# Attention weights built with keys on the partitions from a second set of scores, in a two-layer hybrid trunk

## The chip, the cores and the metric

The kernel runs on one core of a Trainium2 chip. The metric is the device time of one execution in microseconds (us). The engines are named as in the profile: PE (matrix products; PEld is its loading of the stationary operand), DVE (vector), ACT (activation), POOL and SP. The last two, in this kernel, mostly issue DMAs.

## The reference

Two layers on 512 tokens of 1024 features, all float32. Each layer is half a SwiGLU, a mixer and half a SwiGLU, every one on a normalised input and added to the stream. The mixer makes one projection of the normalised input, splits its columns over three groups (a short convolution, a gated recurrence, and attention) and projects the joined results back. The change is in the attention, which is this, for 8 heads of 64 features:

```python
qh = rms_norm(heads(q), q_gain) * (HEAD_DIM ** -0.5)
kh = rms_norm(heads(k), k_gain)
vh = heads(v)
log_f = jax.nn.log_sigmoid((f_logit + f_bias).astype(f32))
cum = jnp.cumsum(log_f, axis=1).transpose(0, 2, 1)
# for each block of 128 queries:
s = einsum('bhqd,bhkd->bhqk', qb, kh) + (cb[..., :, None] - cum[..., None, :])
s = jnp.where(qpos[:, None] >= kpos[None, :], s, MASK_VALUE)
p = jax.nn.softmax(s, axis=-1)
o = einsum('bhqk,bhkd->bhqd', p, vh)
```

The term `cb` is the same for all keys of a query, so it does not change the softmax; only minus `cum` of the key is needed.

## The kernel before, in words

Products are made at float32 accuracy out of float32r ones: every operand is split into a rounded part and a remainder (`hi` and `lo`, `PH` and `PL`, `yh` and `yl`), and the product is the sum of high by high, high by low and low by high. The dense products (`mm3`, lines 376, 382 and 383) do this with three matmuls each. Weight rows come by DMA into `st` (2 buffers), ACT writes the high part and DVE the remainder into `hl` (3 buffers, lines 362 and 363), and PE multiplies.

A layer's mixer begins with the recurrence (`hgrn`), beside which the columns q, k of the attention are projected (`fox_qkv`). Then comes the stretch that the change touches, in which two generators are interleaved by hand. One is `rest()`: what is left of the projection of v, the convolution (`conv`), and most of the output projection (`most`). The other is `attend`, made by `fox_attend`. The tuple `BESIDE` says how many steps of `rest()` stand before each step of `attend`; a step of `rest()` is 12 matmuls of 512 columns in the convolution and 9 in the output projection. `follow("p", ...)` fixes the order of most of these matmuls on PE. The tile scheduler orders the other engines.

`attend` takes the 8 heads in two steps each: p = 0 for the first two blocks of 128 queries, p = 1 for the last two. With causal masking p = 0 has 3 blocks of 128 x 128 and p = 1 has 7.

- `prep(h)` (`fox_prep`) turns q and k of the head by four PE transposes (line 1532), splits them (lines 1535, 1536) and copies the parts by six DMAs on SP's queue into operands: QA, KA (128 rows) and QB, KB (66 rows, of which two are ones in QB, and minus `cum`, split in two, in KB). The memset of the ones is POOL's (line 1529), the DMA of minus `cum` SP's (line 1528).
- `scores(h, p)` makes the scores with queries on the partitions: two products for each query block (all of line 1570) and a mask by a bfloat16 product. DVE takes the maximum (line 1584), ACT the exponential with the sum accumulated (line 300, a helper), DVE the reciprocal, ACT or DVE the scaling (lines 1590, 1592).
- `turn(h, p)` transposes the weights on PE (line 1607), and ACT and DVE split them into `PH` and `PL` (lines 1612, 1613; two buffers each).
- `values(h, p)` multiplies: `V` holds for each head 64 columns of the rounded value and 64 of its remainder, so one matmul of 128 columns against `PH` and one against `PL` give both (line 1625). At p = 1 ACT copies the lower half away and DVE adds the halves into `fo` (lines 1638, 1639); after the odd head of a pair, `fo` is split for the output projection (lines 1642, 1643).

In a step k the order is turn(k), scores(k+2), values(k-1), prep. So the weights have two steps to become ready and the values one more.

PSUM has 8 banks: three `mm` for the dense products, two `sc` for scores, two `pt` for transposes, one `po` for the values.

Of the kernel before, what the change touches and what calls it, by code (L numbers as in the profile page):

```python
# [24 lines left out]
BESIDE = (3, 2, 1) + (1, 1, 2, 1, 1, 2, 2) + (1, 2, 2, 2, 2, 2, 1, 2, 2)  # L25
# [158 lines left out]
class Trunk:  # L184
# [820 lines left out]
    def mix(self, l, w, w_out, conv_w, out_gain, q_gain, k_gain, f_bias, next_gain, logits):  # L1005
# [3 lines left out]
        with tc.tile_pool(name=self.n("mix"), bufs=1) as mp:  # L1009
# [117 lines left out]
            with tc.tile_pool(name=self.n("at"), bufs=1) as ap_:  # L1127
                self.tt, self.tb = "t", 2
# [8 lines left out]
                def conv():  # L1137
                    inv2 = ap_.tile([P, T], F32, tag="t", name=self.n("iv2"), bufs=self.tb)
                    nc.scalar.activation(inv2, inv, AF.Square)
                    for i in range(2):  # L1140
                        bx, bc = yield from features_steps(
                            [(C_X + i * P, P), (C_C + i * P, P)], ("mm", "mm"), **beside
                        )
                        self.conv_in(ap_, i, bx, bc, inv2, cw)
# [43 lines left out]
                assert next(g, "end") == "end"  # L1188
# [13 lines left out]
    def conv_in(self, pool, i, px, pc, inv2, cw):  # L1202
# [14 lines left out]
        self.cy = getattr(self, "cy", {})  # L1217
        self.cy[i] = y
# [238 lines left out]
    def fox_qkv(self, mp, hp, tokens, half):  # L1457
# [44 lines left out]
        V = mp.tile([P, 4, NH, 2, HD], F32R, tag="V", name=self.n("V"))  # L1502
        half.append(V)
        for i, bank in enumerate((yield from beside(tokens((F_V, T), keep=True)))):
            src = bank.rearrange("p (h d) -> p h d", d=HD)
            sc = self.invc[:, i : i + 1]
            nc.scalar.activation(V[:, i, :, 0, :], src, AF.Copy, scale=sc)
            nc.vector.scalar_tensor_tensor(
                out=V[:, i, :, 1, :], in0=src, scalar=sc, in1=V[:, i, :, 0, :],
                op0=ALU.mult, op1=ALU.subtract,  # L1510
            )

    def fox_prep(self, pool, h, qk, g):

        nc = self.nc
        tl = lambda tag: self.mp.tile([P, T], F32R, tag=tag, name=self.n(tag))  # L1520
        hi, lo = tl("b0"), tl("b1")
        if h % 2:
            QA, KA, QB, KB = (tl(t) for t in ("S0", "S1", "q0", "q1"))
        else:
            A = self.mp.tile([P, 2, T], F32R, tag="n", name=self.n("A"))
            QA, KA, QB, KB = A[:, 0, :], A[:, 1, :], tl("kb0"), tl("kb1")
        QB, KB = QB[:66, :], KB[:66, :]
        nc.sync.dma_start(KB[64:66, :].bitcast(F32), self.negc[h])
        nc.gpsimd.memset(QB[64:66, :].bitcast(F32), 1.0)
        b = self.bank("pt")  # L1530
        for i in range(4):
            self.follow("p", nc.tensor.transpose(
                b[:, i * P : (i + 1) * P], qk[:, i, h % 4].rearrange("p w d -> p (w d)"), self.ident
            ))
        nc.scalar.activation(hi, b, AF.Copy, scale=g)
        nc.vector.scalar_tensor_tensor(
            out=lo, in0=b, scalar=g, in1=hi, op0=ALU.mult, op1=ALU.subtract
        )
        for to, src in (
            (QA[:64], hi[:64]), (KA[:64], hi[64:]), (KA[64:], hi[64:]), (QB[:64], hi[:64]),  # L1540
            (QA[64:], lo[:64]), (KB[:64], lo[64:]),
        ):
            nc.sync.dma_start(to.bitcast(F32), src.bitcast(F32))
        return QA, QB, KA, KB

    def fox_attend(self, pool, half, g):


        nc = self.nc
        tl = lambda tag, n: pool.tile([P, T], F32, tag=tag, name=self.n(tag), bufs=n)  # L1550
        E = lambda i: self.follow("p", i)
        ops, weights, turned = {}, {}, {}
# [4 lines left out]
        def scores(h, p):  # L1557
            QA, QB, KA, KB = ops[h]
            pb = pool.tile([P, (384, 896)[p]], F32, tag=f"P{p}", name=self.n("P"), bufs=2)
            s2 = lambda tag: pool.tile([P, 2], F32, tag=tag, name=self.n(tag), bufs=2)  # L1560
            nm, rs = s2("nm"), s2("rs")
# [5 lines left out]
            for u in range(2):  # L1567
                i = 2 * p + u
                c, n = slice(i * P, (i + 1) * P), (i + 1) * P
                mm = lambda *a, **k: E(nc.tensor.matmul(*a, skip_group_check=True, **k))  # L1570
                mm(at[u], QA[:, c], KA[:, :n], start=p == 1 or u == 0, stop=False)
                mm(at[u], QB[:, c], KB[:, :n], start=False, stop=False)
                if p == 1:
                    mm(at[u][:, c], self.identb, self.maskb, start=False, stop=True)
                elif u == 1:

                    mm(
                        b.rearrange("p (b t) -> p b t", t=P)[:, ::2, :], self.identb,
                        self.maskb.unsqueeze(1).to_broadcast([P, 2, P]), start=False, stop=True,
                    )  # L1580
            to = [pb[:, :P], pb[:, P:]] if p == 0 else [pb[:, : 3 * P], pb[:, 3 * P :]]
            for u in range(2):
                o = slice(u, u + 1)
                nc.vector.tensor_reduce(nm[:, o], at[u], axis=AX.X, op=ALU.max, negate=True)
                self.act(to[u], at[u], AF.Exp, bias=nm[:, o], accum_out=rs[:, o])
            nc.vector.reciprocal(rs, rs)
            for u in range(2):
                o = slice(u, u + 1)
                if p:
                    nc.scalar.activation(to[u], to[u], AF.Copy, scale=rs[:, o])  # L1590
                else:
                    nc.vector.tensor_scalar(to[u], to[u], scalar1=rs[:, o], scalar2=None, op0=ALU.mult)
            weights[h, p] = to

        def turn(h, p):


            to = weights.pop((h, p))
            blocks = [(j, u) for j in range(2 * p + 2) for u in range(2) if j <= 2 * p + u]
            PH, PL = (  # L1600
                pool.tile([P, 7, P], F32R, tag=t_, name=self.n(t_), bufs=2) for t_ in ("PH", "PL")
            )
            for a in range(0, len(blocks), 4):
                some = blocks[a : a + 4]
                tb = self.bank("pt")
                for k, (j, u) in enumerate(some):
                    E(nc.tensor.transpose(  # L1607
                        tb[:, k * P : (k + 1) * P], to[u][:, j * P : (j + 1) * P], self.ident
                    ))
                ph, pl = (x[:, a : a + len(some), :].rearrange("p b t -> p (b t)") for x in (PH, PL))  # L1610
                t = tb[:, : len(some) * P]
                nc.scalar.copy(ph, t)
                nc.vector.tensor_sub(pl, t, ph)
            turned[h, p] = blocks, PH, PL

        def values(h, p):
            blocks, PH, PL = turned.pop((h, p))
            if p == 0:
                self.ob = self.bank("po")
            last = 2 * p + 1  # L1620
            for j in range(last + 1):
                at = [k for k, (jj, _) in enumerate(blocks) if jj == j]
                o = slice((2 * p + 2 - len(at)) * P, (2 * p + 2) * P)
                for part in (PH, PL):
                    E(nc.tensor.matmul(  # L1625
                        self.ob[:, o], half[2][:, j, h].rearrange("p a d -> p (a d)"),
                        part[:, at[0] : at[-1] + 1, :].rearrange("p b t -> p (b t)"),
                        start=j == 0 and part is PH, stop=j == last and part is PL,
                        skip_group_check=True,
                    ))  # L1630
# [3 lines left out]
            if h % 2 == 0:  # L1634
                self.fo = tl("fo", 1)
            fo = self.fo
            ft = tl(self.tt, self.tb)
            nc.scalar.copy(ft[r, :], self.ob[64:, :])
            nc.vector.tensor_add(fo[r, :], self.ob[:64, :], ft[r, :])
            if h % 2:  # L1640
                kt = 4 + h // 2
# [6 lines left out]
        scores(0, 0)  # L1648
        prep(1)
        yield  # L1650
        scores(0, 1)
# [128 lines left out]
```

## Time and profile before

| | us |
|---|---|
| median of 3 runs | 1831.44 (1829.89 to 1835.75) |
| profiled execution | 1831.55, of which the span of the trace is 1829.8 |
| PE busy | 1821.3 |
| DVE busy | 1446.0 |
| ACT busy | 1002.4 |
| POOL busy | 185.1 |

The clock that PE was granted is 1.00 in nearly every part of the span. A line of a timeline gives the start, the time from the first start to the last end, the engine and source line, the operation, and the tiles (written <- read). For matmuls it then gives rows and columns of the stationary operand ("128*64" has 64 columns), and partitions and elements of the moving one. Successive instructions of one kind are merged (x7). PE's instructions overlap, so a matmul's own time is longer than its distance from the next start. Plain float32 matmuls appear as two instructions each.

### The profile page before, as it was taken

The page shows a single profiled execution, that of the slowest core. Times are in us where ns is not written, and L with a number is a line of the kernel's source. Part 1 is how long each engine was busy: PE and PEld are TensorE (multiplying, and loading weights), DVE is VectorE, ACT ScalarE, POOL GpSimd, SP SyncE. Part 2 cuts the span into 40 slices and gives each one's busy share as a digit, 9 for nine tenths or more (in the row PEclk, how much of TensorE's full clock was granted, in tenths as well). Part 3 has the DMA queues.
Part 4 walks back from the last instruction along what each step waited for, and adds up shares of the span by engine and source line. Part 5 has one row for each costly group of instructions (what it writes and reads, how often), then busy time and mean ns, then how long its engine had stood idle before and what let it go on. Part 6 is the DMA issues. An engine that isn't in the chain of part 4 may idle for free.

```text
span 1829.8 us, 32009 instructions
## 1 busy us (share of the span) xinstructions
PE 1821.3 (100%) x12939; PEld 1674.5 (92%) x12939; DVE 1446.0 (79%) x1965; ACT 1002.4 (55%) x1415; POOL 185.1 (10%) x190
## 2 busy tenths in 40 slices
PE   9999999999999999999999999999999999999999
PEld 7899999888888899999889999998888888999997
DVE  7889787679677888878678887976777777888883
ACT  5455554465666465555445555555656655555552
POOL 0011120100000101112001111201000001020210
PEclk9999999999999999999999999999999999999999
DMA  7658784242543767868265787823425438677762
GB/s 209 182 128 193 179 177 97 66 125 69 127 111 97 215 136 169 191 167 174 81 201 138 174 181 192 165 70 79 119 72 127 118 98 221 156 156 196 150 140 92
DMA packets 249908, 262.38 MB, mean 143 GB/s; under 512 B 19816, under 2 KB 228464, under 8 KB 249760
## 3 DMA queue, kind: packets, MB, share of 16 engines
q1 hardware_dynamic: 193344, 191.63, 35.2%
q0 software_dynamic: 55840, 68.19, 23.4%
q8 instruction: 101, 1.65, 0.4%
q10 hardware_dynamic: 576, 0.52, 0.1%
q14 instruction: 47, 0.39, 0.1%
HBM read 226.15 MB, written 2.17 MB: 125 GB/s over the span
## 4 chain that ended last, share of the span: by engine, by line
PE 95%; DVE 2%; ACT 1%; DMA 1%; issue 0%; SPq 0%; DVEq 0%; ACTq 0%
PE mm L376 14%; PE mm L383 14%; PE mm L382 14%; PE sc L376 6%; PE sc L382 6%; PE sc L383 6%; PE pt L382 6%; PE pt L376 6%; PE pt L383 6%; PE po L382 4%; PE po L376 4%; PE po L383 4%; PE sc L1570 1%; PE po L1625 1%; PE sc L1384 1%; PE pt L1607 1%
## 5 line engine op out<-in xcount | busy, mean ns | idle before, releaser
L811 ACT CAST hl<-w 128x1024 fp32r<-128x1024 f32 x322 | 337.8, 1050 | 347.0 <-PE mm L383 83.2
L813 DVE TENSOR_TENSOR hl<-w,hl 128x1024 fp32r<-128x1024 f32 x322 | 393.3, 1223 | 86.5 <-ACT hl L811 86.3
L363 DVE TENSOR_TENSOR hl<-st,hl 128x1024 fp32r<-128x1024 f32 (+3 forms) x152 | 160.3, 1054 | 119.9 <-ACT hl L362 119.5
L362 ACT CAST hl<-st 128x1024 fp32r<-128x1024 f32 (+3 forms) x152 | 138.6, 912 | 174.8 <-PE po L383 83.0
L376 PE MATMUL mm<-xc,hl 128*128 128x256 f32 (+1 forms) x730 | 201.6, 277 | 0.3 <-ACT g L910 0.3
L383 PE MATMUL mm<-xc,hl 128*128 128x256 f32 x728 | 201.6, 277 | 0.0
L382 PE MATMUL mm<-xc,hl 128*128 128x256 f32 x728 | 201.5, 277 | 0.0
L376 PE MATMUL sc<-xc,hl 128*128 128x256 f32 (+1 forms) x530 | 146.5, 277 | 0.6 <-ACT g L910 0.6
L383 PE MATMUL sc<-xc,hl 128*128 128x256 f32 x528 | 146.3, 277 | 0.0
L382 PE MATMUL sc<-xc,hl 128*128 128x256 f32 x528 | 146.1, 277 | 0.0
L376 PEld LDWEIGHTS mm<-xc,hl 128*128 128x128 f32 x730 | 137.1, 188 | 0.8 <-ACT g L910 0.5
L383 PEld LDWEIGHTS mm<-xc,hl 128*128 128x128 f32 x728 | 136.8, 188 | 0.1
L382 PEld LDWEIGHTS mm<-xc,hl 128*128 128x128 f32 x728 | 136.8, 188 | 0.0
L376 PE MATMUL pt<-xc,hl 128*128 128x256 f32 (+1 forms) x482 | 132.8, 276 | 0.0
L382 PE MATMUL pt<-xc,hl 128*128 128x256 f32 x480 | 132.8, 277 | 0.0
L383 PE MATMUL pt<-xc,hl 128*128 128x256 f32 x480 | 132.7, 276 | 0.0
L376 PE MATMUL mm<-x,hl 128*128 128x512 f32 x272 | 108.9, 400 | 0.0
L383 PE MATMUL mm<-x,hl 128*128 128x512 f32 x272 | 106.2, 391 | 0.0
L382 PE MATMUL mm<-x,hl 128*128 128x512 f32 x272 | 106.0, 390 | 0.0
L376 PEld LDWEIGHTS sc<-xc,hl 128*128 128x128 f32 x530 | 99.6, 188 | 1.5 <-ACT g L910 1.0
L383 PEld LDWEIGHTS sc<-xc,hl 128*128 128x128 f32 x528 | 99.2, 188 | 0.1
L382 PEld LDWEIGHTS sc<-xc,hl 128*128 128x128 f32 x528 | 99.2, 188 | 0.0
(483 smaller groups left out, 5480.0 us busy)
## 6 DMA issues: line engine op xcount, KB each, us to landing
w<-in_ffn_w_in_dram SPq DMA_DIRECT2D x140, 512.0 KB
w<-in_ffn_w_out_dram SPq DMA_DIRECT2D x64, 512.0 KB
w<-in_ffn_w_out_dram POOLq DMA_DIRECT2D x56, 512.0 KB, 9.0
st<-in_w_mix_in_dram SPq DMA_DIRECT2D x80, 256.0 KB
w<-in_ffn_w_in_dram POOLq DMA_DIRECT2D x39, 512.0 KB, 8.0
st<-in_ffn_w_in_dram SPq DMA_DIRECT2D x70, 256.0 KB
w<-S POOLq DMA_DIRECT2D x35, 512.0 KB, 4.7
st<-in_ffn_w_out_dram SPq DMA_DIRECT2D x24, 512.0 KB
```

The lines of the kernel that those rows point to most:

```text
L362: a = nc.scalar.copy(hi, src[:, c : c + w])
L363: b = nc.vector.tensor_sub(lo, src[:, c : c + w], hi)
L376: i = nc.tensor.matmul(acc[:, c], ah, bh[:, c], start=first and c.start == 0, stop=False, skip_group_check=True,)
L382: nc.tensor.matmul(acc, ah, bl, start=False, stop=False, skip_group_check=True)
L383: i = nc.tensor.matmul(acc, al, bh, start=False, stop=last, skip_group_check=True)
L811: A(nc.scalar.copy(hi, src))
L813: return lambda: V(nc.vector.tensor_sub(lo, src, hi))
L1384: nc.tensor.matmul(s2[:, :, t], e[:, i * P : (i + 1) * P], e2[:, :, t], start=True, stop=True)
L1570: mm = lambda *a, **k: E(nc.tensor.matmul(*a, skip_group_check=True, **k))
L1607: E(nc.tensor.transpose(tb[:, k * P : (k + 1) * P], to[u][:, j * P : (j + 1) * P], self.ident))
L1625: E(nc.tensor.matmul(self.ob[:, o], half[2][:, j, h].rearrange("p a d -> p (a d)"), part[:, at[0] : at[-1] + 1, :].rearrange("p b t -> p ( ...
```

## The change

The scores are made twice. First (`maxima`), with queries on the partitions, only from the rounded parts and minus `cum`: one product for each query block, and DVE's maximum, negated. POOL's queue writes the 2 x 128 maxima to DRAM and reads them back as a row, row 66 of the operand `Q1`, against ones in row 66 of `K1`. Then (`weights`) the scores are made with keys on the partitions, from `K1`, `Q1` (67 rows: high by high, minus `cum`, minus the maximum) and `K2`, `Q2` (128 rows: the other two parts), with the mask as before. ACT takes the exponential out of PSUM into `E` and rounds it to `PH`, DVE makes `PL`; both have one buffer now. Nothing is transposed.

`V` holds 64 columns of value and 64 of ones for each head, so the products against `PH` and `PL` also give the sums of the weights in the lower half. The remainder of the values lies in `VL` (64 columns), multiplied by `PH` alone, in a third matmul into the upper half. The division is done once for a pair of heads: ACT copies both halves out of PSUM, takes Ln and Exp(-x) of the sums, DVE improves this by one Newton step and multiplies.

The order in a step is values(k-1), weights(k), maxima(k+2), prep. Operands have three sets of buffers. `V`, `VL` and the new operands lie in the attention's pool, `fo` in a resident tile. `BESIDE` adds up to 30 where it was 32, and what is left of `rest()` runs after the last values. The convolution multiplies each input by the norm `inv` on DVE, where ACT copied one and DVE multiplied the other by its square.

```diff
-BESIDE = (3, 2, 1) + (1, 1, 2, 1, 1, 2, 2) + (1, 2, 2, 2, 2, 2, 1, 2, 2)
+BESIDE = (3, 2, 2) + (1, 1, 2, 1, 1, 2, 1) + (1, 2, 1, 2, 1, 2, 1, 2, 2)
...
-                assert next(g, "end") == "end"
+                for _ in g:
+                    pass
...
-        nc.scalar.copy(y, px)
-        nc.vector.tensor_mul(u, pc, inv2)
+        nc.vector.tensor_mul(y, px, self.inv)
+        nc.vector.tensor_mul(u, pc, self.inv)
...
+                V = self.ap_.tile([P, 4, NH, 2, HD], F32R, tag="V", name=self.n("V"))
+                VL = self.ap_.tile([P, 4, NH, HD], F32R, tag="VL", name=self.n("VL"))
+                half += [V, VL]
+                for j in range(4):
+                    nc.gpsimd.memset(V[:, j, :, 1, :].bitcast(F32), 1.0)
...
+        for x in (Q1, K1):
+            nc.gpsimd.memset(x[64:67, :].bitcast(F32), 1.0)
+        nc.sync.dma_start(K1[64:66, :].bitcast(F32), self.negc[h])
...
-                mm(at[u], QA[:, c], KA[:, :n], start=p == 1 or u == 0, stop=False)
-                mm(at[u], QB[:, c], KB[:, :n], start=False, stop=False)
+                mm(at[u], Q1[:66, c], K1[:66, :n], start=p == 1 or u == 0, stop=False)
...
+                nc.vector.tensor_reduce(
+                    nm[:, u : u + 1], at[u], axis=AX.X, op=ALU.max, negate=True
+                )
+            row = self.dram.tile([2, P], F32, tag="nm", name=self.n("nm"), bufs=4)
+            nc.gpsimd.dma_start(row.rearrange("u p -> p u"), nm)
+            nc.gpsimd.dma_start(
+                Q1[66:67, 2 * p * P : 2 * (p + 1) * P].bitcast(F32), row.rearrange("(o u) p -> o (u p)", o=1)
+            )
...
+        def weights(h, p):
+            Q1, Q2, K1, K2 = ops[h]
+            PH, PL = (
+                pool.tile([P, 7 * P], F32R, tag=t_, name=self.n(t_)) for t_ in ("PH", "PL")
+            )
+            for a in range(0, 2 * p + 2, 2):
+                b = self.bank("pt")
+                n = 0
+                for j in (a, a + 1):
+                    q = slice(max(2 * p, j) * P, 2 * (p + 1) * P)
+                    o, c = slice(n, n + q.stop - q.start), slice(j * P, (j + 1) * P)
+                    mm(b[:, o], K1[:67, c], Q1[:67, q], start=j == a, stop=False)
+                    mm(b[:, o], K2[:, c], Q2[:, q], start=False, stop=a < 2 * p and j > a)
+                    n = o.stop
+                if a == 2 * p:
+                    mm(blocks(b), self.maskb, two(self.identb), start=False, stop=True)
+                e = tl("E", 2)
+                self.act(e[:, :n], b[:, :n], AF.Exp)
+                ph, pl = (x[:, a * 2 * P : a * 2 * P + n] for x in (PH, PL))
+                nc.scalar.copy(ph, e[:, :n])
+                nc.vector.tensor_sub(pl, e[:, :n], ph)
+            parts[h, p] = PH, PL
...
+                v = V[:, j, h].rearrange("p a d -> p (a d)")
+                mm(self.ob[:, q], v, PH[:, o], start=j == 0, stop=False)
+                mm(self.ob[:, q], v, PL[:, o], start=False, stop=False)
+                mm(
+                    self.ob[:64, q], VL[:, j, h], PH[:, o],
+                    start=False, stop=j == last,
+                )
...
+            nc.scalar.copy(fo[r, :], self.ob[:64, :])
+            nc.scalar.copy(fs[r, :], self.ob[64:, :])
             if h % 2:
+                x = tl("E", 2)
+                self.act(x, fs, AF.Ln)
+                self.act(x, x, AF.Exp, scale=-1.0)
+                nc.vector.tensor_mul(fs, fs, x)
+                nc.vector.scalar_tensor_tensor(
+                    out=x, in0=fs, scalar=-2.0, in1=x, op0=ALU.add, op1=ALU.mult
+                )
+                nc.vector.scalar_tensor_tensor(
+                    out=fo, in0=fo, scalar=-1.0, in1=x, op0=ALU.mult, op1=ALU.mult
+                )
...
         for k, (h, p) in enumerate(steps):
-            turn(h, p)
-            if k + 2 < len(steps):
-                scores(*steps[k + 2])
             if k:
                 values(*steps[k - 1])
+            weights(h, p)
+            if k + 2 < len(steps):
+                maxima(*steps[k + 2])
             if p == 0 and h + 2 < NH:
                 prep(h + 2)
             yield
```

More of the change, by code (lines that the diff above doesn't have):

```diff
@@ L1520, in fox_prep @@
         tl = lambda tag: self.mp.tile([P, T], F32R, tag=tag, name=self.n(tag))
+        own = lambda tag: pool.tile([P, T], F32R, tag=tag, name=self.n(tag))
         hi, lo = tl("b0"), tl("b1")
[L1522 to L1529 removed]
+        if h % 3 == 0:
+            A = self.mp.tile([P, 2, T], F32R, tag="n", name=self.n("A"))
+            Q2, K2, Q1, K1 = A[:, 0, :], A[:, 1, :], tl("kb0"), tl("kb1")
+        elif h % 3 == 1:
+            Q2, K2, Q1, K1 = (tl(t) for t in ("S0", "S1", "q0", "q1"))
+        else:
+            Q2, K2, Q1, K1 = (own(t) for t in ("Q2", "K2", "Q1", "K1"))
+        for x in (Q1, K1):
+            nc.gpsimd.memset(x[64:67, :].bitcast(F32), 1.0)
+        nc.sync.dma_start(K1[64:66, :].bitcast(F32), self.negc[h])
         b = self.bank("pt")
@@ L1550, in fox_attend, with maxima @@
         tl = lambda tag, n: pool.tile([P, T], F32, tag=tag, name=self.n(tag), bufs=n)
-        E = lambda i: self.follow("p", i)
-        ops, weights, turned = {}, {}, {}
+        mm = lambda *a, **k: self.follow("p", nc.tensor.matmul(*a, skip_group_check=True, **k))
+        ops, parts = {}, {}
+        blocks = lambda b: b.rearrange("p (b t) -> p b t", t=P)[:, ::2, :]
+        two = lambda x: x.unsqueeze(1).to_broadcast([P, 2, P])
         def prep(h):
             ops[h] = self.fox_prep(pool, h, half[h // 4], g)
[L1557 to L1561, printed above, removed]
+        def maxima(h, p):
+            Q1, _, K1, _ = ops[h]
+            nm = pool.tile([P, 2], F32, tag="nm", name=self.n("nm"), bufs=2)
             if p == 0:
@@ L1586, in scores @@
[L1586 to L1599, printed above, removed]
+                    mm(blocks(b), self.identb, two(self.maskb), start=False, stop=True)
@@ L1616, in values @@
+            parts[h, p] = PH, PL
         def values(h, p):
-            blocks, PH, PL = turned.pop((h, p))
+            PH, PL = parts.pop((h, p))
+            V, VL = half[2:]
             if p == 0:
                 self.ob = self.bank("po")
-            last = 2 * p + 1
+            n, last = 0, 2 * p + 1
             for j in range(last + 1):
[L1622 to L1630, printed above, removed]
+                q = slice(max(2 * p, j) * P, 2 * (p + 1) * P)
+                o = slice(n, n + q.stop - q.start)
+                n = o.stop
+                v = V[:, j, h].rearrange("p a d -> p (a d)")
[5 more added lines that the diff above has]
+                )
```

59 lines of the change are left out of this document (16 added, 43 removed).

## The prediction

> **What bounds the kernel now.** First the page, parts 1 and 4, then the windows of the two stretches that hold the attention (459 to 593 us in layer 0, 1359 to 1495 us in layer 1).
>
> ```profile
> span 1829.8 us, 32009 instructions
> PE 1821.3 (100%) x12939; PEld 1674.5 (92%) x12939; DVE 1446.0 (79%) x1965; ACT 1002.4 (55%) x1415; POOL 185.1 (10%) x190
> ...
> PE 95%; DVE 2%; ACT 1%; DMA 1%; issue 0%; SPq 0%; DVEq 0%; ACTq 0%
> ...
> 459.00:593.00 134.00, 133.38 (x745) 109.73 (x745) 95.47 (x174) 85.94 (x174) 3.26 (x6) 1.00 0.42 108
> ```
>
> PE is the bound: the chain that ends last is 95% PE, and in the stretch (columns: PE, PEld, DVE, ACT, POOL busy) PE is idle for 0.62 of 134 us, while DVE is busy for 71% and ACT for 64% of it. PE's order is given by hand, so the time changes by the PE time that the edits add or remove, plus any wait that they open. Busy time is no measure of that, since matmuls overlap; I use the distance from one start to the next, read from the timeline of PE. These are the two steps of one head with the stretch of projection products between them cut out:
>
> ```profile
> 503.41 0.93 PE L1607 MATMUL pt<-ident,P 128*128 128x128 f32 x7
> 504.09 0.42 PE L1570 MATMUL sc<-A 128*128 128x384 f32 x1
> 504.35 0.34 PE L1570 MATMUL sc<-kb,kb 66*128 66x384 f32 x1
> 504.53 0.23 PE L1570 MATMUL sc<-maskb,identb 128*128 128x128 bf16 x1
> ...
> 504.89 0.40 PE L1570 MATMUL sc<-kb,kb 66*128 66x512 f32 x1
> 505.13 0.23 PE L1570 MATMUL sc<-maskb,identb 128*128 128x128 bf16 x1
> 505.17 0.36 PE L1625 MATMUL po<-PH,V 128*128 128x256 f32 x1
> 505.37 0.28 PE L1625 MATMUL po<-PL,V 128*128 128x256 f32 x1
> 505.49 0.22 PE L1625 MATMUL po<-PH,V 128*128 128x128 f32 x1
> ...
> 505.66 0.45 PE L376 MATMUL mm<-x,hl 128*128 128x512 f32 x1
> ...
> 508.48 0.49 PE L1607 MATMUL pt<-ident,P 128*128 128x128 f32 x3
> 508.72 0.31 PE L1570 MATMUL sc<-S,S 128*128 128x128 f32 x1
> 508.86 0.27 PE L1570 MATMUL sc<-q,q 66*128 66x128 f32 x1
> 508.98 0.34 PE L1570 MATMUL sc<-S,S 128*128 128x256 f32 x1
> 509.15 0.29 PE L1570 MATMUL sc<-q,q 66*128 66x256 f32 x1
> 509.29 0.28 PE L1570 MATMUL sc<-maskb,identb 128*128 128x256 bf16 x1
> 509.32 0.36 PE L1625 MATMUL po<-PH,V 128*128 128x256 f32 x1
> ...
> 510.29 0.62 PE L1532 MATMUL pt<-ident,qk 128*128 128x128 f32 x4
> ```
>
> Per head that is: transposes 0.68 + 0.24, scores 1.08 + 0.60, value products 0.49 + 0.97; 4.06 us, and 65.0 us for the 16 heads of both layers. A product against 128 loaded columns takes about 0.12 (12 value products in 1.46), whether it moves 128 or 256 columns.
>
> **Maxima.** The first scores keep one product of two. From the step with two blocks go the second products, 508.86 to 508.98 and 509.15 to 509.29: 0.60 - 0.26 = 0.34. From the other go 504.35 to 504.53 and 504.89 to 505.13: 1.08 - 0.42 = 0.66. Together 1.00.
>
> **Weights.** The second scores replace the ten transposes. The step with two key blocks has four products and a mask, which is the group from 508.72 to 509.32: 0.60. The other has four more: 0.60 + 4 x 0.12 = 1.08. Together 1.68. So maxima and weights cost 2.68 where scores and transposes cost 2.60: +0.08 per head, 1.3 us in all.
>
> **Values.** Each pair PH, PL against V gains a third product against VL. VL has 64 columns, V has 128 (value beside ones). That is six more products per head, 96 in all. At their neighbours' 0.12 they would add 0.72 per head, 11.5 us in all, and the sum would stop at +12.8. But they are narrower, and the trace has such products, at L1400, among those of 128:
>
> ```profile
> 458.81 0.39 PE L382 MATMUL po<-hl,x 128*128 128x512 f32 x1
> 459.04 0.39 PE L383 MATMUL po<-hl,x 128*128 128x512 f32 x1
> 459.35 0.33 PE L1400 MATMUL sc<-A,v 128*64 128x128 f32 x2
> ...
> 462.08 0.44 PE L1400 MATMUL sc<-A,v 128*64 128x128 f32 x4
> ...
> 462.57 0.61 PE L1400 MATMUL sc<-A,v 128*64 128x128 f32 x8
> 463.11 0.55 PE L1407 MATMUL sc<-qe,lk 128*128 128x64 f32 x3
> ...
> 426.40 0.39 PE L383 MATMUL po<-hl,x 128*128 128x512 f32 x1
> 426.62 0.49 PE L1384 MATMUL sc<-t,t 128*128 128x128 f32 x3
> ```
>
> Going from 128*128 to 128*64 the next start comes 0.31 after L383 where the stream has 0.23, so 0.08 to 0.09 more; going from L383 to L1384, of the same width 128*128, costs nothing (0.22). L1400 runs in pairs: the eight from 462.57 span 0.61, of which 0.28 is the last pair's own time, so 0.11 per pair; the first four after the change span 0.44, so 0.16 for their one interval, 0.05 more. Going back, 463.11 - 462.57 is 0.54, of which three intervals make 0.33; the fourth is 0.21, 0.10 more. The three L1407 after it span 0.55: less the last one's 0.28 that is 0.14 per interval, where 0.11 is the rule of that run, so another 0.05. One round trip to a narrow product and back thus costs 0.19 at the least and 0.29 at the most, if the two 0.05 do not overlap. I take 0.25, between them. Every VL product stands between wide ones (PH, PL, VL, PH, PL, VL), so each pays the round trip: 96 x 0.25 = 24 us; ends 18.2 and 27.8.
>
> The Trainium skill has the rule in TensorEngine Tiling (Array Packing), Key Properties: changing the tiling mode drains the TensorE. It speaks against this change, and the rows agree in sign. If it means a full drain, the next start waits for the end of the last product (a duration of 0.28 where the distance is 0.12: 0.16 each way, 0.32 per VL, 30.7 us); that is a rival below.
>
> **Waits on PE.** The chain behind the weights is exponential, copy, difference, then the next step's values; the copy of the pair of operands is single now. It is bounded by these groups of this stage:
>
> ```profile
> L1584 DVE TENSOR_REDUCE nm<-sc 128x1 f32<-128x512 f32 x7 | 4.8, 682 | 0.0
> L300 ACT ACTIVATE P<-sc,nm 128x512 f32<-128x512 f32 x7 | 4.8, 680 | 0.0
> L1612 ACT CAST PH<-pt 128x512 fp32r<-128x512 f32 x8 | 4.7, 584 | 4.7 <-PE pt L1607 4.6
> L1613 DVE TENSOR_TENSOR PL<-pt,PH 128x512 fp32r<-128x512 f32 x8 | 5.5, 688 | 3.8 <-ACT PH L1612 3.8
> L1536 DVE SCALAR_TENSOR_TENSOR b<-pt,qkg,b 128x512 fp32r<-128x512 f32 x6 | 4.5, 749 | 0.4 <-ACT b L1535 0.3
> ```
>
> 0.68 + 0.58 + 0.69 = 1.95 us from the first bank to its PL. Cover in the shortest step: the rest of the weights 0.5, maxima 0.66, nine projection products of 0.23 (2.1): 3.3. That leaves 1.3 for what stands ahead on ACT and DVE in their orders (the halves of the next weight rows, the convolution's products). I expect a wait of some 0.5 us in one or two steps per layer, at the end of the convolution, none elsewhere.
>
> The row of maxima goes through DRAM, by two DMAs on POOL's queue, of which the second waits for the first. Nearest:
>
> ```profile
> cw<-in_conv_w_dram POOLq DMA_DIRECT2D x6, 1.0 KB, 3.1
> ...
> row<-inv POOLq DMA_DIRECT2D x2, 2.0 KB, 1.6
> ...
> L1081 POOL DMA_DIRECT2D invc<-row x2: 796/796/796, 358.0 to 1261.0; - x2
> ...
> L1529 POOL MEMSET q<- x8: 519/519/521, 407.2 to 1444.7; 2x512 f32 x8
> ```
>
> The write of 256 single words is like cw: 0.8 to issue, 3.1 to land; reading it back 0.8 and 1.6 to 3.1. With two reductions (the larger 0.68, together about 1.2) that is 7.5 to 9 us from the maxima to the weights two steps later. Cover: two stretches (2.8 each in the convolution, 2.1 the short one after it) and four to five us of attention products: about 10. It just holds, and the narrow products widen it. POOL is held by one pair for 0.8 + 3.1 + 0.8 = 4.7 us a step, with two memsets of 0.52 per head 10.4 us; a head lasts 13 (6.4 of attention products by the sum below, 0.4 for its four transposes from L1532, 27 products of the stream). What queues behind POOL is SP: its DMA of negc into K1 waits for the memset of K1, and behind it on SP are the rows of the projections. Two buffers of rows and three of halves stand ahead of PE, so a delay of a us or two there shows nowhere.
>
> Behind the last pair PE waits already:
>
> ```profile
> 585.26 0.19 PEld L382 LDWEIGHTS sc<-fyl,hl 128*128 128x128 f32 x1 [0.54 <-DVE fyl L1643]
> ```
>
> The new end (two copies, Ln and Exp, three DVE operations, copy, difference: 6.2 us by rows of 0.58 to 0.75) is longer than the old one (2.6) by as much as the two stretches of projection products moved behind it add (18 x 0.23 = 4.1). I leave it as it is, ends -0.5 and +1 per layer. The second pair's result is read 9 us after its values, its chain through busy queues takes as long: 0 to +0.5. New waits 1 to 4, take 2; the early waits of the old scores for the exponential, about 1 us, go. Net +1.
>
> The rest is off PE: the convolution's multiplication by the norm moves from ACT to DVE, and the removed scaling gives both room that nobody waits for. V and VL lie in the attention's own memory now, with POOL's memsets of ones ahead of their first use and DVE's writing of VL behind the first reductions; the convolution's first products need the banks that this empties. They come one stretch later (some 3 us) than the first maxima: 0, and 0.5 if DVE is behind, within the ends of the waits.
>
> **Sum.** 1.3 + 11.5 + 24 + 1 = 37.8. The profiled execution took 1831.55 us for its span of 1829.8, which is the median of the runs (1831.44) to 0.1: 1831.5 + 37.8, about 1869. Own range of this case, with 18.2 to 27.8 for the round trips and 0 to 5 for waits: 1862 to 1877.
>
> **Rivals.**
>
> *The narrow product costs no change of mode.* VL then goes at 0.12 and the time is 1831.5 + 12.8 + 1 = 1845. For it: L1400 also comes from a different number format than VL, which is multiplied like PH and PL. Against: L1407 and L1400 have the same one, and the way back costs as much. Chance 0.13.
>
> *Full drain at every change*, as the rule above would have it: 30.7 in place of 24, 1876. Against: no start in these rows is put off by as much as 0.16. Chance 0.08.
>
> *A new wait takes over.* If ACT or DVE is not free when the first bank is done, or the row through DRAM lands late, each step waits; from 1.3 us of queueing on (0.5 is the usual idle time there) it decides. With 0.5 us in each of the 32 steps: 1869 + 16 = 1885. For it: DVE has its 1.2 us halves in the same queue. Against: 30% of DVE and 36% of ACT are free in this stretch. Chance 0.1.
>
> *The narrow products run beside others.* L1400's pairs are two products in 0.11. If VL, which needs half the columns, went beside its neighbours likewise, a triple would take 3 x 0.055 = 0.17 against 0.23 for today's pair: -0.07 x 96 = -6.7, with the +1.3 and no new wait, against the 1 us that goes: 1825. It decides where a triple takes less than 0.2. Against: PH and PL fill all 128 columns, so there is no free half. Chance 0.03.
>
> That the change does not do what it says is none: the listing of the changed program has the 96 products of tile 128*64 more and 160 transposes fewer.
>
> **Numbers.** Forecast 0.66. About 0.3% (5.5 us) is what this kernel's measurement can tell from no change. Slower: the forecast, the first three rivals, 0.97, less 0.02 for a first rival in which VL hides as well: 0.95. Same 0.02. Faster 0.03. The range reaches down to the first rival's upper end, 1846, and up into the third's, 1882; outside are most of the first (0.1), the upper half of the third (0.05) and the last (0.03).
>
> **What would show it.** Right: L1400-like rows for the VL products in the values group, with starts 0.2 after PL and the next PH 0.2 or more after VL; the values of a head at 3.3 to 3.7 us where they were 1.46; PE still busy throughout, without idle time ahead of weights or values; maxima 1.0 and weights 1.7 per head. Wrong: triples of 0.36 (then 1845), or idle PE ahead of the values for DVE or ahead of the weights for a DMA (then 1880 and more), or a clock below 1.00 in the stretch.

## The result and the profile after

The changed kernel took 2001.82 us (median of 4, 1992.98 to 2008.52) against 1830.87 us: the ratio is 1.0926, 95% interval 1.0909 to 1.0943. It is 171 us slower; 38 were forecast, and the range ended at 1882.

The page of the changed kernel, parts 1, 2 and 4, and the window that was shown of the kernel before (columns: PE, PEld, DVE, ACT, POOL busy, granted clock, DMA share, GB/s):

```profile
span 1999.4 us, 32310 instructions
...
PE 1875.4 (94%) x13035; PEld 1721.0 (86%) x13035; DVE 1442.3 (72%) x1913; ACT 992.2 (50%) x1329; POOL 236.5 (12%) x278
...
PE   9999999998667899999999999999986679999999
...
PEclk9999999999877999999999999999997879999999
...
459.00:593.00 134.00, 96.15 (x491) 80.09 (x490) 57.85 (x92) 46.69 (x77) 20.07 (x35) 0.83 0.40 73
```

PE is no longer busy throughout: in the window it works 96 of 134 us where it worked 133, and it gets through 491 products where it got through 745. Its clock there is 0.83, before it was 1.00. Both happen only in the two attention stretches, slices 10 to 14 and 30 to 33. What PE waits for, in the list of waits (total us, times, longest):

```profile
PE pt L1560 <- DMA q<-nm: 46.5, 9, 9.6
PE pt L1560 <- DMA Q<-nm: 36.0, 6, 9.1
PE pt L1560 <- DMA kb<-nm: 24.2, 8, 5.9
PE mm L376 <- DVE xT L1161: 5.3, 2, 2.8
```

The first three are one wait: the weights (tile pt) for the row of maxima (nm) that comes back from DRAM into Q1, which lies in q, Q or kb by turns. They make 106.7 us in 23 of the 32 steps. POOL's timeline shows why, and below it stand the source lines of the write and of the read (POOL instructions, and issue to landing: minimum, median, maximum):

```profile
530.90 0.54 POOL L1593 DMA_DIRECT2D Q<-nm  x1 [9.69 <-DMA nm<-nm]
531.43 0.98 POOL L1536 MEMSET q<- 3x512 f32 x2
532.36 0.74 POOL L1592 DMA_DIRECT2D nm<-nm  x1
541.99 0.54 POOL L1593 DMA_DIRECT2D Q<-nm  x1 [8.89 <-DMA nm<-nm]
542.52 0.74 POOL L1592 DMA_DIRECT2D nm<-nm  x1
```

```profile
L1592 POOL DMA_DIRECT2D nm<-nm x32: 711/744/753, 479.5 to 1629.0; - x32
...
DMA to landing us min/median/max: 8.0/9.5/11.1
```

```profile
DMA to landing us min/median/max: 1.7/3.3/7.2
```

The write of 1 KB lands after 9.5 us. POOL waits for that before it issues the read, and only then the next write: a step takes POOL 10 to 11 us (532.36 to 542.52), a head 20 to 22, where PE needs 13. From the last reduction of a step to its weights it is 17.6 us in the median of the 32 steps.

The second loss is the clock. This is PE behind one such wait:

```profile
534.47 1.11 PE L1560 MATMUL pt<-Q,K 67*128 67x256 f32 x4 [6.00 <-DMA Q<-nm]
...
537.57 0.63 PE L382 MATMUL mm<-x,hl 128*128 128x512 f32 x1
537.99 0.50 PE L383 MATMUL mm<-x,hl 128*128 128x512 f32 x1
538.33 0.39 PE L376 MATMUL mm<-x,hl 128*128 128x512 f32 x1
538.56 0.40 PE L382 MATMUL mm<-x,hl 128*128 128x512 f32 x1
...
540.41 0.27 PE L1560 MATMUL po<-PH,V 128*128 128x256 f32 x1
540.52 0.28 PE L1560 MATMUL po<-PL,V 128*128 128x256 f32 x1
540.64 0.28 PE L1560 MATMUL po<-PH,VL 128*64 128x256 f32 x1
540.76 0.22 PE L1560 MATMUL po<-PH,V 128*128 128x128 f32 x1
```

After 6.00 us of waiting, products of 512 columns start 0.42 apart (537.57 to 537.99), and from 538.33 on again 0.23: half speed for 3.9 us. The Trainium skill (TensorE: Matmul & The Clock Gate, Part 1) has this: after an idle window of about 3.4 us the array runs at half its clock, until it has been busy for as long. The trace agrees in kind: half speed lasts 3.9 us here, and 6.7 us behind the wait of 9.07 us that ends at 1538.4. PE's busy time rose by 54 us (1821.3 to 1875.4). In the run `direct` below, which has the same 13035 products and hardly waits, it is 1830.0, so some 45 us are slow products.

The last four rows are the narrow products. PL to VL is 0.12 and VL to the next PH is 0.12: the change of tile, priced at 0.25 in the forecast, is not there.

### The profile page after: what moved, and what is told of

Same layout as the page of the kernel before. It is cut to its first block, busy times and chain, and to the rows that moved or that the text cites. A ratio compares the mean times of both kernels' runs of the same rounds, so it can differ in the third digit from the quotient of the medians.

```text
span 1999.4 us, 32310 instructions
## 1 busy us (share of the span) xinstructions
PE 1875.4 (94%) x13035; PEld 1721.0 (86%) x13035; DVE 1442.3 (72%) x1913; ACT 992.2 (50%) x1329; POOL 236.5 (12%) x278
## 5 line engine op out<-in xcount | busy, mean ns | idle before, releaser
L1588 DVE TENSOR_REDUCE nm<-sc 128x1 f32<-128x128 f32 (+1 forms) x64 | 29.5, 486 | 131.9 <-PE sc L1560 131.2
L376 PE MATMUL mm<-x,hl 128*128 128x512 f32 x272 | 113.9, 419 | 2.1 <-DVE VL L1513 2.1
L382 PE MATMUL mm<-x,hl 128*128 128x512 f32 x272 | 110.1, 405 | 0.0
L383 PE MATMUL mm<-x,hl 128*128 128x512 f32 x272 | 109.2, 401 | 0.0
L376 PEld LDWEIGHTS sc<-xc,hl 128*128 128x128 f32 x530 | 99.5, 188 | 1.5 <-ACT g L910 1.0
L786 POOL DMA_DIRECT2D w<-in_ffn_w_in_dram x39 | 57.6, 1477 | 357.0 <-DMA w<-in_ffn_w_in_dram 201.8
```

The costliest lines, as they stand in the source:

```text
L376: i = nc.tensor.matmul(acc[:, c], ah, bh[:, c], start=first and c.start == 0, stop=False, skip_group_check=True,)
L382: nc.tensor.matmul(acc, ah, bl, start=False, stop=False, skip_group_check=True)
L383: i = nc.tensor.matmul(acc, al, bh, start=False, stop=last, skip_group_check=True)
L786: G(nc.gpsimd.dma_start(raw[u, q], src(u, q2), accum_op=ALU.add))
L1588: nc.vector.tensor_reduce(nm[:, u : u + 1], at[u], axis=AX.X, op=ALU.max, negate=True)
```

## The experiments

Ratios are to the kernel before, measured beside each.

**The row without DRAM** (`direct`). Each half of the row goes from the 128 partitions straight into Q1.

```
-            row = self.dram.tile([2, P], F32, ...)
-            nc.gpsimd.dma_start(row.rearrange("u p -> p u"), nm)
-            nc.gpsimd.dma_start(Q1[66:67, ...], row.rearrange("(o u) p -> o (u p)", o=1))
+            for u in range(2):
+                c = slice((2 * p + u) * P, (2 * p + u + 1) * P)
+                nc.gpsimd.dma_start(Q1[66:67, c].bitcast(F32), nm[:, u : u + 1])
```

> No DRAM: each half of the row goes by its own DMA on POOL's queue from the 128 partitions of the maxima straight into Q1[66:67] (128 single words each). Theory 1: POOL waits for no landing, so its queue is free; time 1848 to 1870. If the single words and not the write to DRAM make the 9.8 us, a landing is still 5 to 9 us, which two steps of 6.5 cover. If the landing is 2 to 3 us it was the write to DRAM. Theory 3 or a clock that falls for another reason: over 1900.

1851.53 us, ratio 1.0106 (1.0089 to 1.0123). The source line of these DMAs, and PE's longest waits:

```profile
DMA to landing us min/median/max: 1.9/2.0/4.0
```

```profile
PE mm L376 <- DVE xT L1161: 6.2, 2, 3.1
PE mm L376 <- DVE VL L1513: 2.1, 2, 1.1
```

All waits for the row are gone, and with them 150.3 of the 171 us. By the two profiles 105 us of that is PE's idle time (124.0 to 19.2) and 45 its busy time. The single words are not slow by themselves: 128 of them into neighbouring words of one row of SBUF land in 2.0 us.

**The row known beforehand** (`shift_row`), and with it the tile change taken away (`shift_wide`). In the first the row of forget sums stands in place of the maxima's; in the second the third value product takes V once more in place of VL.

```
-            (the two DMAs of the row)
+        nc.sync.dma_start(Q1[66:67, :].bitcast(F32), self.negc[h, 0:1])     # once per head
```

```
-                mm(self.ob[:64, q], VL[:, j, h], PH[:, o], start=False, stop=j == last)
+                mm(self.ob[:, q], v, PH[:, o], start=False, stop=j == last)
```

> The row in Q1[66:67] is no longer made from the maxima: it is the row of forget sums, one DMA per head on SP's queue, known before the attention begins. Maxima products and reductions still run, their result is unused; the exponential takes a tenth of the score. Theory 1 (POOL's queue is the bound: each write of the maxima takes 9.8 us to land and holds the read and the next write behind it, 10.8 us a step; the clock falls only because PE stands idle): no wait for a DMA left ahead of the weights, granted clock 1.00, and the PE work of the changed kernel alone is left: 1831.5 + 1.3 + 96 x 0.09 to 0.12 + waits of 3 to 7, so 1846 to 1852. Theory 2 (the price of tile changes as predicted, 0.25 each): 1869 to 1876. Theory 3 (the exponential, copy and difference with single halves are late too, masked so far by the row): 1860 to 1890 with PE idle ahead of the values for DVE.

> As the run with the row of forget sums, and the third value product takes V (128 columns) in place of VL (64), so that no tile changes; the remainder of the values is left out and its place filled by a second PH product. Theory 1 (a narrow product costs no change of tile): the same time as with VL within 2 us. Theory 2 (0.25 for each round trip): 18 to 28 us less than with VL.

1854.68 (1.0123, 1.0108 to 1.0139) and 1854.60 us (1.0126, 1.0111 to 1.0141). The first lies 3 us above what was expected, but bears out `direct`: without the round trip the loss is 20 us or a little more, not 171. The second shows that the narrow tile costs nothing: from its first to its last start, the longer group of value products takes 1.22 us with VL and 1.24 with V.

**Queue or latency** (`act_write`, `ahead3`, `ahead3_act`). The write on ACT's queue; the maxima three steps ahead (the tile nm then has three buffers); both.

```
-            nc.gpsimd.dma_start(row.rearrange("u p -> p u"), nm)
+            nc.scalar.dma_start(row.rearrange("u p -> p u"), nm)
```

```
-            if k + 2 < len(steps):
-                maxima(*steps[k + 2])
+            if k + 3 < len(steps):
+                maxima(*steps[k + 3])
```

> Only the write of the maxima to DRAM goes from POOL's queue to ACT's; the read stays on POOL. Theory 1 (it is the queue that holds the next write behind the last one's landing): POOL's step falls from 10.8 us to the spacing of PE; what stays is the latency of one row, 9.8 + 0.5 + 3.3 = 13.6 us against two steps of 6.5, so 1 to 2 us of waiting a step and a clock near 1.00: 1870 to 1920. Theory 1b (the latency of the row alone sets the time, the queue does not): over 1960, as now. Theory 3: nothing changes, 1990 to 2005.

> The changed kernel with the maxima made three steps ahead of their weights and not two; both DMAs on POOL. If the latency of one row (17.5 us from the reduction to the weights) is the bound, three steps cover it and the time falls to 1860 to 1890. If POOL's queue is (one write's landing, one read and one write at a time, 10.8 us a step) it stays near 1990: 16 steps x 10.8 = 173 us a layer either way.

> Three steps ahead, and the write on ACT's queue, so that neither a write nor a read holds the next write behind it. By either of the two bounds (queue, latency) this is the one in which both are gone: 1852 to 1880. If it stays over 1950, the reads themselves (issue to landing 5 to 12 us with the write on ACT) or ACT's order are the bound.

2019.48 (1.1012, 1.0969 to 1.1055), 1972.59 (1.0754, 1.0724 to 1.0783) and 1967.04 us (1.0727, 1.0708 to 1.0746). My theory that POOL's queue alone was the bound falls with the first: writes leave 0.2 us after the last reduction where they left 4.1 after it (medians), and it is no faster, since from that reduction to the weights it is still 18.8 us (17.6 before). Three steps ahead fits neither answer, and both together do not help either. PE's waits in `ahead3` show what took the place, and three rows of SP's queue stand below them:

```profile
PE sc L1560 <- DMA kb<-b: 23.5, 3, 11.0
PE sc L1560 <- DMA S<-b: 23.3, 4, 7.9
PE pt L1560 <- DMA kb<-nm: 19.5, 3, 8.8
PE sc L1560 <- DMA Q<-b: 11.7, 2, 5.9
```

```profile
SPq L1537 <- POOL kb L1536: 42.4, 6, 10.7
SPq L1537 <- POOL q L1536: 31.6, 4, 10.6
SPq L1537 <- POOL K L1536: 24.5, 4, 11.0
```

Now the maxima (tile sc) wait for SP's copies of the operands (b), which three steps ahead have one step to land where they had two. These copies never touch DRAM, and PE waits up to 11.0 us for one of them. There are two ways to that. One is POOL's queue: the memset of an operand (L1536) stands behind the wait for the landing, SP's DMA of minus `cum` (L1537) waits for the memset, and the copies stand behind it on SP; these waits make 98.5 us here and 13.5 in `direct`. The other is that the slow write holds up the transfers themselves, which the next run tries.

**Writes that nobody reads** (`spectator`): `direct`, with the old write and a second one of 128 words beside it.

```
+            row = self.dram.tile([3, P], F32, ...)
+            nc.gpsimd.dma_start(row[0:2].rearrange("u p -> p u"), nm)
+            nc.gpsimd.dma_start(row[2:3].rearrange("u p -> p u"), nm[:, 1:2])
```

> The maxima go straight into the row (as in the run without DRAM, 1851.5), and beside it the same 256 words and once more 128 of them are written to DRAM, where nobody reads them. Theory A (a scattered write to DRAM costs only those who wait for its landing): 1851 to 1858, the landing of the unused writes 8 to 10 us. Theory B (it also holds up the other transfers, as the longer landings of SP's copies and of the reads suggest): the copies of operands and the rows of the projections land late and PE waits for them, 1870 to 1960.

1907.72 us, ratio 1.0417 (1.0398 to 1.0436): 56 us more than `direct`, for writes of 1.5 KB a step whose result is not used. Among PE's waits:

```profile
PE pt L1560 <- DMA Q<-nm: 8.1, 2, 4.3
PE pt L1560 <- DMA kb<-nm: 7.5, 3, 6.1
PE sc L1560 <- DMA Q<-b: 5.8, 2, 4.2
PE sc L1560 <- DMA S<-b: 3.4, 1, 3.4
PE sc L1560 <- DMA q<-b: 3.0, 1, 3.0
```

Theory B holds in kind: rows and copies that need no DRAM are late again, and POOL's queue waits for none of these writes. Not all of the 56 us need be late transfers: nm has two buffers, and 7 times DVE's reduction waited for an unread write to give one back (16.5 us in all). The DMA share shows the burden. This is the window 459 to 593 us in `direct` and in `spectator`:

```profile
459.00:593.00 134.00, 129.17 (x753) 108.64 (x752) 84.19 (x135) 72.72 (x121) 25.08 (x48) 0.99 0.41 105
```

```profile
459.00:593.00 134.00, 116.97 (x640) 97.13 (x637) 74.29 (x121) 61.22 (x104) 43.51 (x77) 0.92 0.68 89
```

The DMA engines are busy for 0.68 of the time, where it was 0.41, and move less (89 GB/s against 105). In the changed kernel the share had stayed at 0.40, but for 73 GB/s where the kernel before moved 108 with 0.42.

**What is slow in the write** (`half_row`, `spread`, `spread64`). One block's 128 words in place of 256; then all 256, but 512 B or 64 B apart in DRAM where they were 4 B apart (k is 128 or 16). The read, not printed here, then takes the same single words. In `half_row` the other block's shift is left out.

```
-            row = self.dram.tile([2, P], F32, ...)
-            nc.gpsimd.dma_start(row.rearrange("u p -> p u"), nm)
+            row = self.dram.tile([2, P, k], F32, ...)
+            nc.gpsimd.dma_start(row[:, :, 0].rearrange("u p -> p u"), nm)
```

> The changed kernel with one of the two blocks' maxima sent through DRAM, 128 single words in place of 256; the other block's shift is left out, and the exponential takes a tenth of the score. If the landing of the write goes with the number of words, it falls from 9.8 to 5 or 6 us, POOL's step to about 7, and the time to 1870 to 1900. If it is a fixed price of such a write, 9 us or more and 1980 to 2000.

> The changed kernel with each word of the row 512 B from the next in DRAM, written and read as single words. If the 9 us come from neighbours that are written into the same piece of DRAM by several DMA engines, the landing falls to 2 to 4 us, POOL's step to 5 to 7 and the time to 1855 to 1890. If every small write to DRAM from 128 partitions takes 9 us, 1985 to 2020, later if the read of single words is slower too.

> The changed kernel with the words of the row 64 B apart in DRAM (4 B in the changed kernel: 9.5 us to landing; 512 B: 2.1 us). If words collide that lie in one piece of 64 B or less: 2 to 2.5 us and 1850 to 1857 as with 512 B. If the pieces are larger (up to 512 B), the landing lies between, 3 to 8 us, and the time between 1856 and 1980.

1972.08 (1.0757, 1.0739 to 1.0775), 1853.38 (1.0120, 1.0101 to 1.0138) and 1853.21 us (1.0113, 1.0097 to 1.0129). The landings of the write, from the source lines of `half_row` and of `spread64`:

```profile
DMA to landing us min/median/max: 6.8/8.6/9.5
```

```profile
DMA to landing us min/median/max: 2.0/2.1/4.1
```

Half the words at the same distance land hardly sooner (8.6 against 9.5), and the time of `half_row` lies outside both ranges, next to that of a fixed price. All of the words 64 B apart land in 2.1. So neither the number of words nor DRAM by itself is the price, but single words written next to each other in DRAM.

`spread64` also gives the cleaner test of the transfers beside the write, since only the distance of the words differs. Where the profile has the landing of SP's copies of the operands (11 of 96, the same ones), it is this in the changed kernel and in `spread64`:

```profile
DMA to landing us min/median/max: 2.3/7.0/9.7
```

```profile
DMA to landing us min/median/max: 2.3/2.9/4.6
```

From the issue on, with every wait of SP's queue behind them, the copies take 7.0 us beside the dense writes and 2.9 beside the spread ones. The Trainium skill (DMA: Bandwidth & Descriptors, Specifications) says that transfers under 512 B are made by reading, changing and writing back. By that alone the words 64 B apart would be as slow as those at 4 B; here a distance of 64 B is enough, and no run tried one between 4 and 64 B. Why neighbouring words are slow stays open.

**Filling the waits** (`filler`): the changed kernel with dense products ahead of each step's weights.

```
+                for _ in range(12 if a == 0 else 0):
+                    mm(b, K2[:, :P], Q2, start=True, stop=True)
```

> The changed kernel with 12 dense products of 512 columns more ahead of the weights of every step; they wait for nothing that comes through DRAM and their result is overwritten. By themselves they are 32 x 12 x 0.227 = 87 us of PE. Theory 1 (PE waits for the row, and the half clock after a long wait is only the price of standing idle): most of them fall into the waits, the waits get shorter than the 3 us or so from which the clock drops, and what was lost to the half clock (150 us of loss less 107 of waiting) comes back: 1975 to 2020 with a clock of 0.98 or more. Theory 2 (the clock is lowered by something else, or PE is the bound): 2060 to 2090, the clock as before.

2001.79 us (1.0915, 1.0899 to 1.0931), the changed kernel's time to 0.03 us, with some 87 us of products more. The same stretch, 459 to 680 us, of the changed kernel and of this one:

```profile
459.00:680.00 221.00, 160.17 (x787) 133.26 (x786) 92.57 (x146) 79.25 (x129) 27.89 (x48) 0.82 0.34 65
```

```profile
459.00:680.00 221.00, 196.66 (x988) 162.16 (x985) 98.76 (x153) 83.29 (x135) 28.00 (x48) 0.93 0.39 67
```

The clock rises from 0.82 to 0.93 as PE stands idle less, so it follows the waits. That more work at a better clock changes nothing in the time shows more: the row, and neither PE's work nor its clock, sets the time of the changed kernel. The 105 and 45 us above say where PE loses time, not what each would give back alone.

**The other 20 us** (`direct_noVL`, `direct_nodiv`, `direct_tail`). From `direct`: the third value product left out; the division left out (the result stays unnormalised); the division of the first three pairs made one step later.

```
+            if h % 2 and h < NH - 1:
+                late.append(lambda: divide(h, fo, fs))
...
+            while late:
+                late.pop(0)()
             if k:
                 values(*steps[k - 1])
```

> The run without DRAM (1851.5), and the third value product, the remainder of the values, left out: 96 products on 128*64 less. At the distances read in the changed kernel's trace (a group of 12 takes 1.22 us where the old 8 took 0.86, a group of 6 0.52 where 4 took 0.38; with the product ahead of each group 0.5 to 0.7 per head) the time falls by 8 to 11.5, to 1840 to 1843.5. At the price predicted for the tile changes it would fall by 35, to 1817.

> The run without DRAM, and the division by the sums left out (two functions on ACT, three operations on DVE per pair of heads; the result is not normalised). If the 3.1 us in which PE waits for a bank at the end of each layer's convolution (the sums into the residual queue behind the division on DVE) come from the division, they go: 1851.5 - 6 = 1845 to 1846. If they come from the halves and from the order of the stretches, 1850 to 1852.

> The run without DRAM (1851.5), and the division of each of the first three pairs of heads made one step later, so that in DVE's order the sums into the residual come before it; the last pair's stays. If the division costs by its place, the 3.1 us of PE's wait per layer go and the time is 1844 to 1846.5. If it costs by its work on DVE and ACT, 1850 to 1853.

1843.00 (1.0059, 1.0044 to 1.0074), 1841.81 (1.0057, 1.0040 to 1.0074) and 1839.37 us (1.0040, 1.0025 to 1.0055). VL costs 8.5 us, 0.09 for each of the 96 products. The division costs by its place: made later it takes 12.2 us off, no less than without it (9.7). Both gain more than was expected, 5 to 7.5 and about 6. In `direct` its end looked like this, DVE first, then PE in layer 0 and in layer 1:

```profile
564.70 0.68 DVE L1654 SCALAR_TENSOR_TENSOR E<-fs,E 128x512 f32<-128x512 f32 x1
565.30 0.95 DVE L363 TENSOR_TENSOR hl<-st,hl 128x768 fp32r<-128x768 f32 x1
566.17 0.68 DVE L1657 SCALAR_TENSOR_TENSOR fo<-fo,E 128x512 f32<-128x512 f32 x1
566.77 1.28 DVE L1161 TENSOR_TENSOR xT<-mm,xT 128x512 f32<-128x512 f32 x2
```

```profile
567.51 0.80 PE L376 MATMUL mm<-hy,hl 128*128 128x512 f32 x1 [3.09 <-DVE xT L1161]
568.10 0.63 PE L382 MATMUL mm<-hy,hl 128*128 128x512 f32 x1
568.53 0.63 PE L383 MATMUL mm<-hy,hl 128*128 128x512 f32 x1
...
1480.70 0.50 PE L376 MATMUL mm<-hy,hl 128*128 128x512 f32 x1 [3.09 <-DVE xT L1161]
1481.04 0.39 PE L382 MATMUL mm<-hy,hl 128*128 128x512 f32 x1
1481.27 0.39 PE L383 MATMUL mm<-hy,hl 128*128 128x512 f32 x1
```

The sums into the residual (xT), which free PE's banks, queue on DVE behind three operations of the division. PE waits 3.09 us and then, in layer 0, runs at half speed (568.10 to 568.53 is 0.43; the granted clock from 567 to 571 us is 0.57). In layer 1 an equal wait leaves the speed whole (1481.04 to 1481.27 is 0.23). Between the profiles of `direct` and `direct_tail` PE's idle time falls by 8.1 us and its busy time by 3.1.

**A version under the time before** (`lean`): `direct_tail` with only the first value product and without DVE's making of PL; weights and values are then used rounded once, which is less exact than both kernels.

```
-                mm(self.ob[:, q], v, PL[:, o], start=False, stop=False)
-                mm(self.ob[:64, q], VL[:, j, h], PH[:, o], start=False, stop=j == last)
```

> No DRAM, the division later, and of the three value products only the first: weights and values are used rounded once (PL and VL left out), sums from the same rounded weights. Against the kernel before 6 value products a head are gone as well: 1851.5 - 8.5 (VL) - 8 to 11 (PL) - 0 to 6 (division later): 1826 to 1835, under the time before if the division's place counts.

1820.04 us, ratio 0.9936 (0.9919 to 0.9953): below 1831 and below the lower end expected. The gain is the products left out; with the arithmetic of the change as it stands, the best is `direct_tail`, 0.4% above the kernel before.

## Why the prediction was wrong, point by point

- **The row through DRAM** is the step that failed: "The write of 256 single words is like cw: 0.8 to issue, 3.1 to land". cw is a read from DRAM, and the one write among the rows, row<-inv (1.6), goes from one partition; this was a write of single words next to each other from 128 partitions, and landed in 9.5. "POOL is held by one pair for 4.7 us a step" became 10 to 11, "7.5 to 9 us from the maxima to the weights" became 17.6, against a cover of about 10. The sum had nothing for it, and it cost 150 us: PE idle for 105 us more and slower products for 45. With words 64 B apart the assumption is right (2.1 to land, time 1853).
- **The rival "a new wait takes over"** named the mechanism (late landing, idle PE ahead of the weights for a DMA), but at 0.5 us a step. It was 3.3 a step over all 32, and no rival counted the slower products behind long waits. Of the signs listed for "wrong", triples of 0.35, idle PE ahead of the weights for a DMA and a clock below 1.00 were all seen.
- **Tile changes**: 24 us expected, none measured, by `shift_wide` and by starts 0.12 apart. What the 0.08 to 0.10 read at L1400 belong to was not tried; L1400 also has another number format, as the first rival said. The first rival was right: with VL at about 0.1 and the row repaired the time is 1851 to 1853, where it said 1845.
- **VL's products**: 11.5 at a full 0.12; 8.5 measured.
- **Maxima and weights**: +1.3 expected. 1839.37 for `direct_tail`, less 8.5 for VL, is 1830.9 against 1831.8 before, so about -1 for all that is left.
- **The end of the convolution**: net +1 was expected of all waits, with "0.5 us in one or two steps per layer". The division's place costs 12.2. I looked at what PE waits for in the attention and not at what the division stands ahead of on DVE. The moved V and VL (2.1 in two waits) and the single halves (0.8) stayed small, as argued. SP behind POOL's memsets, put at "a us or two", stayed small only in the repaired kernels: SP waited 13.5 us for them in `direct`, 68.6 in the changed kernel.

Added up: 150.3 for the row, 12.2 for the division's place, 8.5 for VL, -1 for the rest: 170, of 171 measured.

## What to carry to other kernels

A transfer is priced by a row of the same direction and layout: single words written next to each other in DRAM are their own case, and putting them 64 B apart, or going from SBUF to SBUF, is a repair of a few lines. A long wait of PE costs more than its length when products behind it run at half speed: in the two repairs the span fell by 1.4 times the idle time that went (150 for 105, and 11.2 for 8.1). Of a step that moves, ask on each engine what it now stands ahead of, not only what it waits for.

## What the runs showed of the hardware

- 256 words written to DRAM 4 B apart from 128 partitions land in 9.5 us (8.3 by ACT's queue), 128 of them in 8.6, 256 of them 64 B or 512 B apart in 2.1; 128 words into one row of SBUF in 2.0.
- Such writes delay other DMAs, those between SBUF tiles too: copies of operands land in 7.0 us beside them and in 2.9 beside words 64 B apart. Writes that nobody reads cost 56 us, of which a buffer that they held may be a part.
- A wait of 3.09 us halved PE's speed behind it in one layer and left it whole in the other; the idle window that the Trainium skill (TensorE: Matmul & The Clock Gate, Part 1) gives, about 3.4 us, is a little longer.
- A product on 128*64 among products on 128*128 starts 0.12 after and before them, like its neighbours.
